# Attention on one core: the order of all steps from a new search, longer products on GpSimd, its casts under VectorE's SBUF steps, and bits and factors in rings

## The chip, the core and the metric

The kernel runs on one core of one Trainium2 chip. The metric is the device time of one execution in microseconds, here the median of 3 runs of the kernel before. The engines are called as the profile calls them: PE is TensorE (with PEld, its weight loads), DVE is VectorE, ACT is ScalarE, POOL is GpSimd, SP is SyncE, which issues most transfers.

## The reference

Grouped-query attention without a mask: 8 batches, 8 query heads and 2 key/value heads, 1,024 positions, 64 columns. That makes 64 query heads ("heads" below), four of which share one key/value head.

```python
q: (8, 8, 1024, 64)   k, v: (8, 2, 1024, 64)   # float32, drawn with deviation 0.1
scores = (1 / sqrt(64)) * q_group @ k_group.transpose
attn = exp(scores - scores_max);  attn = attn / (sum(attn) + 1e-8)
output = attn @ v_group
```

The kernel leaves the maximum out (the scores are small) and divides after the second product: a column of ones beside v gives the sum.

## The kernel before, in words

**Tiles of scores.** Keys are cut into 8 chunks of 128, so a head has 8 score tiles of 128 keys by 1,024 queries; there are 512 in all. PE makes a tile with two matmuls of 512 columns (L761) into one of three PSUM slots of two banks each (`sp`). A slot is free again when its tile has been read.

**Two ways to the exponential.** 368 tiles go to ACT, one instruction each (L771, "exponential"), which writes bf16 tiles `pt`. The other 144 go to VectorE, which makes the exponential from bits. Its steps, with the names used below:

- *pass* (L783): scores from PSUM, scaled and shifted, written as 16-bit whole numbers `yt`, 1,024 columns a tile
- *bits* (L792): the low seven bits of `yt` and a fixed exponent, to `zt`
- *exponent* (L800): the high bits of `yt`, to `et`
- *product* (L810 on VectorE, L739 on GpSimd): `zt = yt * zt`, read as bf16; the columns are split between the two engines, GpSimd takes pieces from the end ("parts")
- *sum* (L816): `zt = et + zt`, only in the last three heads; elsewhere PE adds `et` and `zt` by using both as weights

Bits, exponent and product run on a *chain* of two tiles (2,048 columns), SBUF to SBUF. Each chain has three buffers of its own, from pools of 6 (`yt`), 8 (`et`) and 8 (`zt`).

**Second product.** PE multiplies `pt`, `et` and `zt` (128 queries at a time, as weights) with v and its column of ones (L829; L849 for the first head, L869 for the last), 65 columns an instruction, into two PSUM banks in turn (`ops`). Seven query pieces of 128 fill a bank. VectorE then takes the *reciprocal* of the sums (L894) and *normalizes* (L904) into `ost`, and SP stores a head when it is complete (L913).

**Loads.** GpSimd casts q, k and v from float32 to bf16 in DRAM with DMAs of its own queue (L519, two heads of q or one batch of k or v a time). SP transposes q and k into SBUF from there (L588, L578) and copies v (L571).

**What sets the order.** Every engine runs its list in order. The lists come from a planner (class `Plan`), which walks through a string of letters, `ORDER`, with a cost for each step, and gives each step a time; it also decides on GpSimd's parts by the room that it sees under VectorE's PSUM steps (`gpsimd`, L207) and on the time of the casts (`due`, L159). The events are sorted by these times and emitted. Waits follow from the data. Two kinds are added by hand: a part of GpSimd waits until the VectorE step ahead of the latest SBUF step has ended (`gate`), and a one-column memset (`tick`, L734) takes a chain's waits for its buffers ahead of its first part.

Of the kernel before, what the change touches and what calls it, by code (L numbers as in the profile page):

```python
# [10 lines left out]
M_START = 5450  # L11
M_KREST = 50
M_SWAP = 650
M_Q1 = 3400
M_QSTEP = 2700
M_WARM = 6400
M_V0 = 8000
M_DUMMY = 110
M_SEE = 51
M_PAIR = 226  # L20
M_PTAIL = 205
M_SWITCH = 99
M_MM = 30.3
M_PVTAIL = 180
M_ACT = 917
M_ATAIL = 107
M_FIX = 66
M_DTAIL = 80
M_DEP = 34
M_D1 = 1.042  # L30
M_D2 = 0.521
M_D4 = 0.261
M_REC = 115
M_GLEAD = -55
M_GDMA = 20
M_ZLEAD = 33
M_GFIX = 190
M_GCOL = 1.88
M_GOVER = 65
M_GLATE = 900  # L40
M_GFREE = 85
M_ISSUE = 850
M_OVER = 5000
NEED = 5150
M_NORM = 531


INF = float("inf")
PB = 7
# [3 lines left out]
CHN = 2  # L53
LONG = 6
GFROM = 2
GTO = 5
GMIN = 64
GREST = 64
GSTEP = 8
STEPS = (("zh", M_D4), ("two", M_D4), ("mul", M_D2), ("add", M_D2))  # L60


ORDER = """
AaApFFFFWWWWFFAWWWWWWWWWWWWWWWWWWWWaWWWWWWWWWWApEEWWEA0bWWWApEFFWWWAW0WWWaEpAEWWA0WWAWWWWWWAFFF0FE0E
WW0WbAWWWWWWWWApWWWWWWWWWWWWAWWRWWnWaWWRWWWPWWAVVVVVVAnb0VVVApVVVVVVA0WaVApVVVVVVVA0AV0bVRVVPVVVAVVV
nVVAb0WWWWApVVVVVVVVAR0WbWWWA0VVVVPVVVVAVVVnVVA0bWWWApVVVVVVVVAR0bWWWA0VVVVPVVVVAVVVnVVA0bWWWApVVVVV
VVVA0AW0WWbVV0VVVVVARPVVVVVVAnWWbWAipVVVVVVVVA1cWWWApVVVVVVVVAr1bWWWA0VPVVVVVVAWWnWWWcWA1VVVVVpVVVAV
VVVRV1AcnWWWAVpVVVVVAVV01VAc1VVVVpVVAVVVVVRA0cWWWWAPVVVVVVVVAnWbWWWA1VVVVpVVAVVVVVRV1VAcnWWWAVpVVVVV
VVA2WWcWWAVpVVVVVVVARWW0nWcWAVpVVVVVVVA1WcWWApVVVVVVVVA00cWWWAVVVVV0VAVRVPVVVAVVVVnVVAA0VVVV1VVVVVVV
1cAV0VVVVVVVRApVVVVVVVAnWcWWAipVVVVVVVVA1cWWWApVVVVVVVVAR0b0WWWAVPVVVVVVVAnWWcWWA1VVVVpVVVVAVVVRV1Ac  # L70
WnWWWWWAVpVVVVVVVA01WWcWApVVVVVVAV1VVVVVRV0AcWWWAPVVVVVVVVAncWW1WAVVVpVVVVVAVVV0VARc0VVVVPVAVVVVVVAn
cWW1WWAVVVpVVVVVVAVV0VVVVA0bWWRWWAPVVVVVVVVnVAc1WAVVpVVVVVVVAW1WWWbAVpVVVVVVVARW0nWcWWApVVVVVVVVA1Wb
WWWApVVVVVVVVA0cRV1AVPVVVVVAVVVnVAA0VVVVV1VVVVVVV0VbAVpVVVVVVAVRV1VVAc1VVVVVPAVVVVVVAnbWWW0WAVpVVVVV
VVAVVRV1VVAc1VVVVVPAVVVVVVVAnbW0WWAVpVVVVVVVArWW1WbWAVPVVVVVVVAnWWcWA1VVVVVpVVAVVVVA01AV1VVVVVVRVnbW
AVpVVVVVVVA0WWbWAVpVVVVVVVVARWW1WbWAVPVVVVVVVVAVnVb0AVpVVVVVAVVVV0VcA1VVVVApVVVVVVA1bVVrAPVVVVVVAnbW
WWW0WApVVVVVVVVA1bWWWARPVVVVVVVVVAnbWW0WAVpVVVVVVVVVA1WWbWA0VVVVVVpVVAVVVVVA0AVRV1VVAVnVVVV0VVVVVb0A
VVVVVpVVVAVVVAR0aVPVVVAVVVVVVnVAb1WWWAVpVVVVVVVVVARWW0Wa0WAVVPVVVVVVVAVnVVVA1AVVV1VVVVVVV0VbAVpVVVVV
VVVARWWnWaWAVpVVVVVVVVVA1WbWWAVpVVVVVVVVARWnWbWWAVpVVVVVVVA01WWaWA0VVVVVpVVVAVVVA1bVRV0pVAVVVVVVnAa1
WWWWAVpVVVVVVVAW1WWWbAVpVVVVVVVARW0WbWWAPVVVVVVVVVAnbWA1VVVV0VVVApVVVVVVVARWW1WbWAVPVVVVVVVVVAVnAb0V
VVVpVVVAVVVVVVrA0nAV1VVVVVVV0bWApVVVVVVVVA0WbWWWApVVVVVVVVAR1WAWWWbV0VVVVPVVVAVVVVnVAb0WWWApVVVVVVVV  # L80
A1bWWWARVPVVVVVVVAnWWbWWA0VVVV0VVVApVVVVVVAR1AVVVnVVVVa0AVpVVVVVVAV0VVVVA0bVRVPVVVAVVVVVnAa1WWWWAVpV
# [10 lines left out]
VVVVVVVVA0WbWWWApVVVVVVVArnAVV2VVVVVV1cAVpVVVVVVVVARWWnWcWAVVpVVVVVVAVV3VVAA00VV0VVVVVVVV0VVAAVVVRV0  # L92
VVVVVV0VVVVVVAanWWWWAVpVVVVVVVVARnbWAVpVVVVVVVVA0Wb0WWWApVVVVVVVVAR0AWWWb0VVVVVPVVVAVVVVnVAb0WWWAVpV
VVVVVVARWW0WAWAVVVVVV0VVVVVVVAAVnVVVVV0VVVVVVVRVA0WAVnVVVVV0VVVVVVVVVVVVVA0AVVVVVVVVVRVnVVVVaApVxVVV
AVVVV0VVVVVRVAnAWA0VV0VVVVVVVV0VVLLRLnLLLLLFFRFn
"""


# [849 lines left out]
```

## Time and profile before

| what | value |
|---|---|
| median of 3 runs | 352.83 us (352.61 to 352.95) |
| span of the profiled execution, first to last instruction | 350.8 us |
| median over that span | 2.0 us |
| granted clock of TensorE | 0.998 |
| busy: PE, DVE, ACT, POOL | 342.2, 340.5, 342.3, 276.9 us |
| exponentials on ACT | 368, busy 339.8 us |
| first exponential starts, last one ends | 6.05 and 345.95 us |
| passes on DVE | 144, busy 174.9 us |
| products on POOL, on DVE | 151 and 64, busy 238.3 and 39.1 us |

The page shows the span of the profiled execution; what lies outside its first and last instruction is seen only as the difference to the median. Busy time counts instructions that overlap on an engine once. The next instruction on VectorE or ACT starts while the one ahead still drains, so the duration of an instruction (1.22 us for a pass) is longer than the time from its start to the next start (1.13), and the latter is what it costs.

### The profile page before, as it was taken

The numbers are of one execution on the slowest core, as the hardware profiler recorded it, in microseconds if no ns is written. First come the engines' busy times: TensorE is split into PE (matmuls) and PEld (weight loads), VectorE is DVE, ScalarE is ACT, GpSimd is POOL, SyncE is SP. The second block draws the span as 40 slices with busy tenths as digits, with TensorE's granted clock in tenths as the row PEclk, the third lists the DMA queues.
The fourth block names the chain that finished last, engine by engine and source line by source line (L and its number), as shares of the span: only waits on it lengthen the run. The fifth ranks groups of instructions, "written<-read, shape, count | busy, mean of one in ns | idle before, by whom it ended". The sixth has DMA issues, their size and how long they took to land.

```text
span 350.8 us, 14254 instructions
## 1 busy us (share of the span) xinstructions
PE 342.2 (98%) x6272; PEld 224.9 (64%) x6272; DVE 340.5 (97%) x517; ACT 342.3 (98%) x372; POOL 276.9 (79%) x265
## 2 busy tenths in 40 slices
PE   7899999999999999999999999999999999999995
PEld 3466666666666666666666666666666676666674
DVE  5999999999999999999999999999999999999995
ACT  6999999999999999999999999999999999999994
POOL 3268889799999999898999998999989958982000
PEclk9999999999999999999999999999999999999999
DMA  6899766496749757769896977297767994453223
GB/s 150 121 165 167 140 120 146 84 151 139 136 92 137 148 124 134 129 132 124 125 157 120 151 138 122 64 191 135 122 127 107 170 168 119 107 122 74 69 76 109
DMA packets 96574, 44.84 MB, mean 128 GB/s; under 512 B 61168, under 2 KB 95344, under 8 KB 95728
## 3 DMA queue, kind: packets, MB, share of 16 engines
q1 hardware_dynamic: 94128, 31.34, 43.8%
q0 software_dynamic: 2096, 12.19, 26.5%
q8 instruction: 49, 0.80, 1.1%
q10 hardware_dynamic: 288, 0.39, 0.3%
q14 instruction: 13, 0.11, 0.1%
HBM read 27.13 MB, written 28.97 MB: 160 GB/s over the span
## 4 chain that ended last, share of the span: by engine, by line
PE 60%; ACT 21%; DVE 15%; issue 1%; DMA 1%; DVEq 0%
PE ops L829 32%; PE sp L761 27%; ACT pt L771 21%; DVE yt L783 8%; DVE et L800 2%; DVE ost L904 2%; DVE zt L792 1%; DVE zt L810 1%; DMA q<-in_q_dram 1%; PE sp L869 1%; DVE rec L894 1%; PE sp L644 0%; DVE qt L662 0%; ACT q L633 0%; DVEq L943 0%
## 5 line engine op out<-in xcount | busy, mean ns | idle before, releaser
L771 ACT ACTIVATE pt<-sp 128x1024 bf16<-128x1024 f32 x368 | 339.8, 1036 | 0.5 <-PE sp L761 0.3
L739 POOL TENSOR_TENSOR zt<-yt,zt 128x560 bf16<-128x560 bf16 (+15 forms) x151 | 238.3, 1583 | 28.3 <-DVE zt L792 10.1
L829 PE MATMUL ops<-va,pt 128*128 128x65 bf16 x2840 | 177.0, 194 | 0.0
L783 DVE TENSOR_SCALAR yt<-sp 128x1024 uint16<-128x1024 f32 x144 | 174.9, 1215 | 1.3 <-PE sp L761 1.2
L761 PE MATMUL sp<-qt,kt 64*128 64x512 bf16 x1024 | 168.9, 382 | 3.2 <-ACT pt L771 1.7
L829 PEld LDWEIGHTS <-pt 128*128 128x128 bf16 x2840 | 131.5, 97 | 32.8 <-issue 32.8
L829 PE MATMUL ops<-va,zt 128*128 128x65 bf16 x1128 | 131.1, 194 | 0.0
L829 PE MATMUL ops<-va,et 128*128 128x65 bf16 x1096 | 125.3, 194 | 0.0
L829 PEld LDWEIGHTS <-et 128*128 128x128 bf16 x1096 | 87.9, 98 | 15.2 <-issue 15.0
L829 PEld LDWEIGHTS <-zt 128*128 128x128 bf16 x1128 | 91.2, 97 | 9.6 <-issue 9.2
L761 PEld LDWEIGHTS <-kt 64*128 64x128 bf16 x1024 | 50.9, 93 | 59.0 <-issue 36.0
L792 DVE TENSOR_SCALAR zt<-yt 128x2048 uint16<-128x2048 uint16 (+1 forms) x73 | 49.8, 683 | 0.5
L800 DVE TENSOR_SCALAR et<-yt 128x2048 uint16<-128x2048 uint16 (+1 forms) x73 | 49.0, 675 | 0.0
L904 DVE TENSOR_TENSOR ost<-ops,rec 128x448 f32<-128x448 f32 (+2 forms) x73 | 44.7, 612 | 0.5
L810 DVE TENSOR_TENSOR zt<-yt,zt 128x928 bf16<-128x928 bf16 (+17 forms) x64 | 39.1, 611 | 0.0
L519 POOL DMA_DIRECT2D qd<-in_q_dram x33 | 21.6, 655 | 4.4 <-PE sp L761 3.6
L894 DVE RECIPROCAL rec<-ops 128x7 f32<-128x7 f32 (+2 forms) x73 | 14.5, 199 | 0.1
L734 POOL MEMSET tick<- 128x1 bf16 x57 | 12.0, 211 | 0.0
L519 POOL DMA_DIRECT2D kd<-in_k_dram x8 | 5.3, 657 | 5.1 <-PE sp L761 5.1
L621 PE MATMUL ops<-warm 128*128 128x128 bf16 (+1 forms) x24 | 4.6, 334 | 1.2 <-DVE warm L513 1.2
L519 POOL DMA_DIRECT2D vd<-in_v_dram x8 | 5.6, 700 | 0.0
L621 PEld LDWEIGHTS <-warm 128*128 128x128 bf16 x24 | 2.0, 114 | 3.5 <-issue 2.3
(39 smaller groups left out, 27.4 us busy)
## 6 DMA issues: line engine op xcount, KB each, us to landing
out_dram<-ost SPq DMA_DIRECT2D x63, 256.0 KB, 3.1
qd<-in_q_dram POOLq DMA_DIRECT2D x29, 256.0 KB, 5.0
kt<-kt SPq DMA_DIRECT2D x30, 64.0 KB, 3.4
va<-vd SPq DMA_DIRECT2D x30, 64.0 KB, 3.1
kd<-in_k_dram POOLq DMA_DIRECT2D x7, 256.0 KB, 4.5
vd<-in_v_dram POOLq DMA_DIRECT2D x7, 256.0 KB, 5.3
qt<-qd SPq DMA_TRANSPOSE x63, 4.5
qd<-in_q_dram POOLq DMA_DIRECT2D x5, 128.0 KB, 4.0
```

What stands on the lines that cost most here:

```text
L519: return nc.gpsimd.dma_start(out=t.rearrange("(a x) d -> a (x d)", a=128), in_=src.rearrange("(a x) d -> a (x d)", a=128),)
L734: early = nc.gpsimd.memset(tick, 0.0)
L739: begun[j] = gps = nc.gpsimd.tensor_tensor(out=z, in0=flat(yt[j])[:, lo : lo + w], in1=z, op=ALU.mult)
L761: now = nc.tensor.matmul(sps[x][:, half, :], lhsT=t[lo : lo + D, c // NH, ci % NH * 128 : (ci % NH + 1) * 128], rhs=qt[j][lo : lo + D, 0, ...
L771: exps.append(nc.scalar.activation(out=p, in_=where_s[(j, c)], func=AF.Exp, scale=scale))
L783: vec = nc.vector.tensor_scalar(out=yt[ch][:, i, :, :], in0=where_s[c], scalar1=EXP_A, scalar2=EXP_B, op0=ALU.mult, op1=ALU.add,)
L792: vec = nc.vector.tensor_scalar(out=zt[j][:, 0:c], in0=yt[j][:, 0:c], scalar1=0x7F, scalar2=0x3F00, op0=ALU.bitwise_and, op1=ALU.bitwise_or,)
L800: vec = ins = nc.vector.tensor_scalar(out=et[j][:, 0:c], in0=yt[j][:, 0:c], scalar1=0x7F80, scalar2=None, op0=ALU.bitwise_and,)
L810: vec = nc.vector.tensor_tensor(out=z, in0=flat(yt[j])[:, 0 : cols[0]], in1=z, op=ALU.mult)
L829: ended[job] = nc.tensor.matmul(ops[plan.group_of[x] % 2][:, lo : lo + D + 1], lhsT=p[:, qs * 128 : (qs + 1) * 128], rhs=va[(b * G + h // ...
L894: vec = nc.vector.reciprocal(out=to, in_=sums)
L904: vec = nc.vector.tensor_tensor(out=to, in0=src, in1=by, op=ALU.mult)
```

## The change

The planner goes. A new string `ORDER`, found by another search, holds the finished order of everything: each score tile with its slot, each exponential, each VectorE step with the chain that it works on, each part of GpSimd with its length in units of 8 columns, and each cast, transpose, copy and store. A loop over its letters emits the instructions directly; two places of it:

```diff
+m2v3A0t2xVVVVVzVTVe1xA2G2,192rpVVVVVxVVVA0nd1xA2pSVVVTVVxVVA0m2q28A1t2xVV
+VVVzVCVe2xG2,195A0rpVVVVVxVVVA1ne2TxA0pSVVVVVxVVVA0m3k7A1zxVVVVVVt4VTVe2xG3,201A0
```

`A` and `a` to `g` are score tiles for ACT and VectorE (the letter counts heads ahead), `x` an exponential, `p` a pass, `z` bits, `t` exponent, `m` VectorE's product, `+` the sum, `G` a part of GpSimd, `V` three or so matmuls of the second product, `r` and `n` reciprocal and normalization, `q`, `k` and `v` casts, `T` a transpose of q, `S` a store. A digit behind `m`, `t` or `G` counts chains back.

The core of the code:

```diff
+NYT = 22
...
-    yp = ctx.enter_context(tc.tile_pool(name="yp", bufs=NYT))
-    ep = ctx.enter_context(tc.tile_pool(name="ep", bufs=NCT))
-    zp = ctx.enter_context(tc.tile_pool(name="zp", bufs=NCT))
...
+    ye = kvp.tile([128, NYT, 2, HS], U16, name="ye")
+    zz = kvp.tile([128, NYT, 2, HS], U16, name="zz")
...
+class Chain:
+    def __init__(self, at, n):
+        self.at, first = at, at % NYT
+        self.first, self.n = first, n
+        self.cols = 1024 * n
+        self.parts = 0
+    def tiles(self, ring):
+        return ring[:, self.first : self.first + self.n]
...
+        elif kind == "z":
+            gate = vec
+            ch = Chain(nzh, lengths[len(chains)])
...
+            vec = nc.vector.tensor_scalar(
+                out=ch.tiles(zz), in0=ch.tiles(ye), scalar1=0x7F, scalar2=0x3F00,
...
+        elif kind == "G":
+            ch = chains[-1 - arg[0]]
+            w = 8 * arg[1]
+            ch.cols -= w
...
+            gps = nc.gpsimd.tensor_tensor(
+                out=z, in0=flat(ch.tiles(ye))[:, ch.cols : ch.cols + w], in1=z, op=ALU.mult
+            )
...
+        elif kind == "t":
+            gate = vec
+            ch = chains[-1 - arg[0]]
+            vec = nc.vector.tensor_scalar(
+                out=ch.tiles(ye), in0=ch.tiles(ye), scalar1=0x7F80, scalar2=None,
+                op0=ALU.bitwise_and,
+            )
```

So `yt` and `et` become one ring `ye` of 22 tiles and `zt` a ring `zz` of 22. The exponent step writes over the tile that it reads. It must therefore come after the product of its chain, VectorE's and GpSimd's, where it had a buffer of its own before. Chains have one or two tiles (`LENGTHS`: 69 of two, 6 of one). The numbers of steps: 368 exponentials and 144 passes as before, 75 bits and 75 exponent steps (73 and 73), 68 products on VectorE with 45,616 columns (64 with 57,912), 95 parts on GpSimd with 101,840 (151 with 89,544), sums over 8 tiles (5), 6,234 matmuls (6,272).

**VectorE in the middle of the program.** Before, around the normalization of one bank; `yt`, `zt` and `et` are the chain's buffers, `sp` a slot of scores, `ops` a bank of the second product, and the brackets hold the semaphores that an instruction waits on (PE, Pool for GpSimd, DVE for VectorE itself, DMA queues):

```order
L783 TENSOR_SCALAR yt<-sp_2742 128x1024 [waits PE_49]
L894 RECIPROCAL rec<-ops_2616 128x7 [waits PE_49]
L792 TENSOR_SCALAR zt<-yt 128x2048 [waits DVE_49]
L800 TENSOR_SCALAR et<-yt 128x2048
L783 TENSOR_SCALAR yt<-sp_2800 128x1024 [waits PE_49,Pool_49]
L904 TENSOR_TENSOR ost<-ops_2616,rec 128x448 [waits DVE_49]
L810 TENSOR_TENSOR zt<-yt,zt 128x640
```

The same engine in the change, over one chain:

```order
L454 TENSOR_TENSOR zz<-ye,zz 128x512
L460 TENSOR_SCALAR ye<-ye 128x2048 [waits DMAHW5_49,DVE_49,Pool_49]
L428 TENSOR_SCALAR zz<-ye 128x2048
L557 RECIPROCAL rec<-ops_2575 128x7 [waits PE_49]
L419 TENSOR_SCALAR ye<-sp_2722 128x1024 [waits PE_49]
L568 TENSOR_TENSOR ost<-ops_2575,rec 128x448 [waits DVE_49]
L419 TENSOR_SCALAR ye<-sp_2766 128x1024 [waits PE_49]
```

Bits and exponent steps that stood between the passes now stand together behind the product, and four PSUM steps stand together. The wait on GpSimd has moved from the pass to the exponent step, which now also waits on VectorE's own product ahead of it.

**GpSimd at the same places.** Before; `tick` is the one-column memset, `qd` and `kd` the casts:

```order
L739 TENSOR_TENSOR zt<-yt,zt 128x560 [waits DVE_49]
L519 DMA kd_0_2626<-in_k_dram 16x8192 [waits DMASW3_49]
L734 MEMSET tick 128x1 [waits PE_49,Pool_49]
L739 TENSOR_TENSOR zt<-yt,zt 128x848 [waits DVE_49]
L519 DMA qd_2694<-in_q_dram 16x8192 [waits DMASW4_49]
```

And in the change:

```order
L445 TENSOR_TENSOR zz<-ye,zz 128x1576 [waits DVE_49]
L172 DMA vd_0_2567<-in_v_dram 16x8192 [waits DMASW6_49]
L440 MEMSET tick 128x1 [waits PE_49,Pool_49]
L445 TENSOR_TENSOR zz<-ye,zz 128x1536 [waits DVE_49]
L172 DMA qd_2686<-in_q_dram 16x8192 [waits DMASW7_49]
```

The parts are longer and fewer, one for each chain here, and a cast stands behind a part, so that it is issued when that part has ended, which is where VectorE's product and exponent step begin.

More of the change, by code (lines that the diff above doesn't have):

```diff
@@ L1 @@
 import math
+import re
 from contextlib import ExitStack
@@ L438, with groups_of @@
+def groups_of(nj):
+    last = (nj - 1) * NPIECE
+    groups = [(0, NPIECE // 2), (NPIECE // 2, NPIECE)]
+    groups += [(i, min(i + PB, last)) for i in range(NPIECE, last, PB)]
+    return groups + [(last, last + NPIECE)]
 @with_exitstack
@@ new lines, in half @@
+    def half(j, par, ci):
+        return [p for _, p in terms(j, par, [ci])]
+    for kind, arg in re.findall(r"([A-Za-z+])([0-9,]*)", "".join(ORDER.split())):
+        arg = [int(x) for x in arg.split(",")] if arg else []
+        if kind == "X":
+            begin("q", arg[0], True)
+        elif kind == "Y":
+            begin("k", divmod(arg[0], G), True)
+        elif kind == "Z":
+            begin("v", divmod(arg[0], G), True)
+        elif kind == "q":
+            begin("q", arg[0], False)
+        elif kind in "kv":
+            begin(kind, (arg[0], 0), False)
+        elif kind == "K":
+            turn_k(*kt_next.pop(0))
+        elif kind == "C":
+            copy_k(*cp_next.pop(0))
+        elif kind == "U":
+            fill_v(*fv_next.pop(0))
+        elif kind == "I":
+            place_v(0, 0)
+        elif kind == "T":
+            turn_q(tq_next)
+            tq_next += 1
+        elif kind == "S":
+            r = place_of(st_next * NPIECE)
+            ins = nc.sync.dma_start(
+                out=rows(out[divmod(st_next, H)], st_next == 0),
+                in_=ost[:, r : r + NPIECE, :].rearrange("p (s two) d -> p s (two d)", two=2),
+            )
+            stores.append(ins)
+            st_next += 1
+        elif kind in "Aabcdefg":
+            while nxt[a] == NC:
+                a += 1
+            j, x = a + (0 if kind == "A" else "abcdefg".index(kind)), arg[0]
+            c = nxt[j]
+            nxt[j] += 1
@@ L828 @@
+            for i in range(ndone, ndone + n):
                 ci, p = every[i]
                 ended[job] = nc.tensor.matmul(
-                    ops[plan.group_of[x] % 2][:, lo : lo + D + 1],
+                    ops[g % 2][:, lo : lo + D + 1],
                     lhsT=p[:, qs * 128 : (qs + 1) * 128],
@@ L873 @@
                         start=(first and i % 4 == 0 and n == 0),
-                        stop=(j == 0 and n == len(every) - 1),
+                        stop=(left_now == 0 and n == len(every) - 1),
                         skip_group_check=True,
                     )
-        elif kind in ("rec", "norm"):
-            lo, hi = x
+            if not left_now:
+                if kind == "E":
+                    pc = NPIECE
+                    norms += groups[:2]
+                else:
+                    norms.append(groups[-1])
+        elif kind in "rn":
+            lo, hi = norms[0]
             n = hi - lo
             r = place_of(lo)
-            if lo < plan.last:
-                o = ops[plan.group_of[lo] % 2][:, 0 : n * (D + 1)]
+            if lo < last:
+                o = ops[group_of[lo] % 2][:, 0 : n * (D + 1)]
                 o = o.rearrange("p (s d) -> p s d", d=D + 1)
```

685 lines of the change are left out of this document (150 added, 535 removed).

## The prediction

> **What bounds the kernel now.** I read the page's busy shares first, then the chain of waits, then the waits by engine, and last the steps of VectorE and GpSimd in order of time.
>
> ```profile
> span 350.8 us, 14254 instructions
> PE 342.2 (98%) x6272; PEld 224.9 (64%) x6272; DVE 340.5 (97%) x517; ACT 342.3 (98%) x372; POOL 276.9 (79%) x265
> ...
> PE 60%; ACT 21%; DVE 15%; issue 1%; DMA 1%; DVEq 0%
> ```
>
> Three engines are at 97 to 98%, and the chain changes hands between them. So one busy share decides nothing, and the question is which engine has idle time inside it. The table of stretches covers the run of exponentials on ACT, from the first to the end of the last:
>
> ```profile
> core 0: us, PE busy (x) PEld busy (x) DVE busy (x) ACT busy (x) POOL busy (x), PEclk, DMA share, GB/s
> 6.05:345.95 339.90, 336.76 (x6226) 222.00 (x6223) 337.20 (x504) 339.75 (x368) 274.88 (x257) 1.00 0.72 127
> ...
> PE sp L761 <- ACT pt L771: 1.7, 5, 0.5
> DVE yt L783 <- PE sp L761: 1.2, 3, 0.5
> ```
>
> ACT is without a gap in this table, and so nearly is everything else. But a gap can hide inside an instruction that starts late while the one ahead drains. Look at where ACT is undisturbed (columns: start, duration, engine, line, operation, tiles):
>
> ```profile
> L771 ACT ACTIVATE pt<-sp 128x1024 bf16<-128x1024 f32 x368 | 339.8, 1036 | 0.5 <-PE sp L761 0.3
> ...
> 332.86 1.02 ACT L771 ACTIVATE pt<-sp 128x1024 bf16<-128x1024 f32 x1
> 339.20 2.02 ACT L771 ACTIVATE pt<-sp 128x1024 bf16<-128x1024 f32 x2
> ```
>
> From 332.86 to 339.20 seven exponentials start, 0.906 us each. Over the kernel they take 339.8/368 = 0.923. So ACT could run 368 x 0.017 = 6.3 us faster: it is held, about 2% of the time, by late scores. The change keeps 368 exponentials, so these 6.3 us are the most that ACT allows. PE loses 38 of 6,272 matmuls, too few to matter. What moves is VectorE, where a step is followed by the next at once nearly everywhere:
>
> ```profile
> 111.92 0.62 DVE L904 TENSOR_TENSOR ost<-ops,rec 128x448 f32<-128x448 f32 x1
> 112.45 0.48 DVE L810 TENSOR_TENSOR zt<-yt,zt 128x640 bf16<-128x640 bf16 x1
> 112.85 1.22 DVE L783 TENSOR_SCALAR yt<-sp 128x1024 uint16<-128x1024 f32 x1
> 113.99 0.20 DVE L894 RECIPROCAL rec<-ops 128x7 f32<-128x7 f32 x1
> 114.11 0.69 DVE L792 TENSOR_SCALAR zt<-yt 128x2048 uint16<-128x2048 uint16 x1
> 114.72 0.69 DVE L800 TENSOR_SCALAR et<-yt 128x2048 uint16<-128x2048 uint16 x1
> 115.32 1.22 DVE L783 TENSOR_SCALAR yt<-sp 128x1024 uint16<-128x1024 f32 x1
> ```
>
> From start to start: normalization 0.53, product of 640 columns 0.40, pass over scores 1.14, reciprocal 0.12, bits 0.61, exponent 0.60. There is no hole. I therefore make the sum on VectorE and hand its change to the end, as long as it stays inside ACT's 6.3.
>
> **The change, part by part.** *Product columns.* GpSimd's parts fall from 151 to 95 and carry 101,840 columns where they carried 89,544. VectorE's own product falls from 57,912 to 45,616 columns.
>
> ```profile
> L810 DVE TENSOR_TENSOR zt<-yt,zt 128x2048 bf16<-128x2048 bf16 x8 | 9.7, 1209 | 0.0
> ...
> L810 DVE TENSOR_TENSOR zt<-yt,zt 128x640 bf16<-128x640 bf16 x8 | 3.8, 476 | 0.0
> ...
> 344.40 0.69 DVE L816 TENSOR_TENSOR zt<-et,zt 128x1024 bf16<-128x1024 bf16 x1
> 345.00 0.19 DVE L894 RECIPROCAL rec<-ops 128x6 f32<-128x6 f32 x1
> ```
>
> A column costs (1209 - 476)/1408 = 0.521 ns, so 12,296 columns are **-6.40 us**. The 640-column step of 0.40 leaves 0.07 as its fixed part. There are four products more (68 for 64), and two bits and two exponent steps more (75 for 73, columns equal): eight fixed parts, **+0.55**. The last heads sum their two factors in 8 tiles instead of 5, one step of 1024 more (0.60, above) and one of 2048 (0.60 + 0.53 = 1.13): **+1.73**. Steps alone: -4.1.
>
> *Waits of VectorE on its own last step.* Here the in-place factors enter.
>
> ```profile
> 161.83 0.20 DVE L894 RECIPROCAL rec<-ops 128x7 f32<-128x7 f32 x1
> 162.06 0.62 DVE L904 TENSOR_TENSOR ost<-ops,rec 128x448 f32<-128x448 f32 x1
> 162.60 1.21 DVE L783 TENSOR_SCALAR yt<-sp 128x1024 uint16<-128x1024 f32 x1
> 163.85 0.76 DVE L792 TENSOR_SCALAR zt<-yt 128x2048 uint16<-128x2048 uint16 x1
> ```
>
> The normalization right behind its reciprocal starts 0.23 after it, not 0.12. The bits step right behind its own pass starts 1.25 after it, not 1.14. So a neighbour that depends costs about 0.117. The built program of before has 34 such neighbours (15 pass to bits, 16 reciprocal to normalization, 3 product to sum). The change has 9 of these three kinds (2, 6 and 1 exponent to sum), but the exponent step now overwrites the tile that the product reads, and in 39 places it stands right behind that product and waits for it. No row shows this wait. [...] I take 0.117, the nearest rows. (48 - 34) x 0.117 = **+1.6**; the ends are -2.9 and +2.9.
>
> [...]
>
> The exponent step also waits for GpSimd's part on its tile. I cost it at nothing: VectorE's rest of the product, some 0.34 for 520 columns, lies between, and GpSimd overlaps it by less, as the next rows show. [...] The wait that the score pass had on GpSimd is gone; nothing was seen to stand there.
>
> *Longer parts.* Of the 95 parts 47 are over 1,300 columns, typically 1,528, started under an exponent or bits step and running through reciprocal, pass, normalization, pass.
>
> ```profile
> 270.45 0.20 DVE L894 RECIPROCAL rec<-ops 128x7 f32<-128x7 f32 x1
> 270.57 1.18 DVE L783 TENSOR_SCALAR yt<-sp 128x1024 uint16<-128x1024 f32 x1
> 271.66 0.61 DVE L904 TENSOR_TENSOR ost<-ops,rec 128x448 f32<-128x448 f32 x1
> 272.19 0.30 DVE L810 TENSOR_TENSOR zt<-yt,zt 128x296 bf16<-128x296 bf16 x1
> 272.41 0.69 DVE L792 TENSOR_SCALAR zt<-yt 128x2048 uint16<-128x2048 uint16 x1
> 273.05 1.22 DVE L783 TENSOR_SCALAR yt<-sp 128x1024 uint16<-128x1024 f32 x1
> ...
> 112.62 1.42 POOL L739 TENSOR_TENSOR zt<-yt,zt 128x560 bf16<-128x560 bf16 x1
> 113.99 0.91 POOL L519 DMA_DIRECT2D qd<-in_q_dram  x1
> ...
> 270.05 2.24 POOL L739 TENSOR_TENSOR zt<-yt,zt 128x904 bf16<-128x904 bf16 x1
> 272.25 0.94 POOL L519 DMA_DIRECT2D qd<-in_q_dram  x1
> ...
> 273.25 3.44 POOL L739 TENSOR_TENSOR zt<-yt,zt 128x488 bf16<-128x488 bf16 x2
> ```
>
> The 560-column part ends at 114.04, 1.19 after the pass at 112.85 opened its window. The 904 columns end at 272.29, 1.84 after the reciprocal. That is 0.65/344 = 1.89 ns a column, so 1,528 end 1.84 + 624 x 1.89 ns = 3.02 after the reciprocal. The four steps last 0.12 + 1.09 + 0.53 + 1.14 = 2.88. The part reaches 0.14 into VectorE's next step. What does that cost? At 272.19 an overlap of 0.10 cost nothing: 296 columns took 0.22, their 0.07 + 0.15. Longer is seen here:
>
> ```profile
> 164.70 4.04 POOL L739 TENSOR_TENSOR zt<-yt,zt 128x560 bf16<-128x560 bf16 x2 [0.58 <-DVE zt L792]
> ...
> 168.60 0.73 DVE L792 TENSOR_SCALAR zt<-yt 128x2048 uint16<-128x2048 uint16 x1
> 169.25 1.21 DVE L783 TENSOR_SCALAR yt<-sp 128x1024 uint16<-128x1024 f32 x1
> ```
>
> An overlap of 0.14 (to 168.74) made the bits step 0.65 long, 0.05 over its usual 0.60. Bounds: 0 and 0.05. I take 0.03, the middle, times 47: **+1.4**, with ends 0 and 2.4.
>
> *Transfers.* GpSimd starts most of its 256 KB casts behind a part, under VectorE's product, exponent and bits steps. Their landing is early enough: each transpose that reads them is issued twelve exponentials (11 us) ahead of its first score, as before. The time goes to GpSimd itself, 0.5 to 0.9 an issue, while it would idle. From the product's start to the next window there are 0.34 + 0.12 + 0.60 + 0.61 = 1.67; part tail 0.14 and issue 0.94 fit. I take 0; the cost without this cover is the slower rival.
>
> *Rings, run of scores, end.* 22 + 22 tiles replace 12 + 16 + 16, and the margins between a tile's last reader and its next writer are over ten exponentials in the order. I cost them, and the tail with its one more sum ahead of the last eight matmuls, at nothing (0.3 either way).
>
> **Sum:** -6.40 + 0.55 + 1.73 + 1.6 + 1.4 = -1.1. The profiled span of 350.8 becomes 349.7. The shown median, 352.83, stands 2.0 above that span; I leave the 2.0 as it is: **351.7 us**.
>
> **The rivals.** *More.* The 39 waits are free, VectorE saves 4.6 more, and ACT's 6.3 just hold it: 351.7 - 4.6 = 347.1. For it: nothing is read back after the product. Against it: the program has the semaphore, and every neighbour with one in these rows pays. 9%.
>
> *No change.* VectorE's saving turns into waits for PE. It is the order that couples the three engines, and ACT's 6.3 us of lateness show that work saved on one does not reach the others by itself: 352.8. Against it: VectorE has the fewest holes of the three. 22%.
>
> *Slower.* GpSimd is late at its window. At 272.25 the issue started 0.16 before a bits step, lasted 0.94, past that step's end at 273.05, and the next part began at 273.25, 0.2 inside the pass. In the order of the change 22 casts stand between VectorE's product and an exponent or bits step. If issue and the small memset behind it are held through both steps, a 1,528-column part starts 0.2 late and reaches 0.34 into the next product, which then waits the added 0.2: 22 x 0.2 = 4.4, or 356.1; half of them 353.9. It decides from about 0.1 of lateness. Against it: at 113.99 two such steps followed, the issue took 0.91 and ended under the second, free before the window. 22%.
>
> [...]
>
> **Chances.** Forecast 47%, of which 5% end within 0.2%; more 9%; no change 22%; slower 22%. A change of 0.2%, 0.7 us, is about what this kernel's measurement can tell. Faster: 42 + 9 = 51%; same: 5 + 22 = 27%; slower 22%. The forecast's own range, from the two ends of the overlap and the tail, is 350.0 to 353.0. For 8 in 10 I take 349.8 to 354.0: below it lies the free wait, above it half of the slower rival.
>
> **What would show it.** Exponent steps 0.117 late behind their product (product of 520 columns to exponent 0.46, not 0.34); 1,528-column parts of about 3.4 us ending 0.14 into the next step; VectorE's steps adding up to 1.1 less; exponentials nearer 0.920 than 0.923 apart. Casts that end inside a pass would show the slower rival. I am wrong if VectorE shows new holes ahead of its passes, since then the order and not the work decides.

## The result, and the profile after

The change makes the kernel slower: 408.29 us (median of 4, 404.82 to 410.01) against 352.89 for the kernel before on the same chip, a ratio of 1.156 with a 95% interval of 1.151 to 1.161. The forecast was 351.7, with 349.8 to 354.0 for 8 in 10. Here and below medians are over all runs of a kernel, ratios and their intervals over its fast runs alone (those within 1.5% of its fastest), so the two can differ a little. From the page of the kernel after, its first rows and two groups, ACT's exponentials and VectorE's exponent steps (the last column is the idle time ahead of the group and what ended it):

```profile
span 403.0 us, 14111 instructions
PE 353.5 (88%) x6234; PEld 227.4 (56%) x6234; DVE 377.8 (94%) x527; ACT 346.0 (86%) x372; POOL 274.6 (68%) x206
...
L407 ACT ACTIVATE pt<-sp 128x1024 bf16<-128x1024 f32 x368 | 343.4, 1052 | 47.7 <-PE sp L396 46.2
...
L460 DVE TENSOR_SCALAR ye<-ye 128x2048 uint16<-128x2048 uint16 (+1 forms) x75 | 86.9, 1163 | 3.5
```

The same group, the exponent step, on the page of the kernel before:

```profile
L800 DVE TENSOR_SCALAR et<-yt 128x2048 uint16<-128x2048 uint16 (+1 forms) x73 | 49.0, 675 | 0.0
```

ACT, which idled 0.5 us ahead of its exponentials before, idles 47.7 now, 46.2 of it for scores. VectorE looks busier, 377.8 us for 340.5, and one group alone grew by 37.9: 75 exponent steps take 86.9 us, where 73 took 49.0. The waits by engine of the kernel after (us in total, times, the longest) show the way from there to ACT:

```profile
ACT pt L407 <- PE sp L396: 46.2, 33, 3.5
PE sp L396 <- DVE ye L419: 33.4, 15, 3.1
POOL zz L445 <- DVE ye L460: 27.4, 15, 5.3
...
DVE ye L419 <- PE sp L396: 12.7, 14, 2.7
```

Some 15 times PE waits up to 3.1 us for a pass of VectorE to free a slot of scores, ACT then waits for PE, GpSimd for the exponent step, and VectorE's next passes for PE in turn. It is not spread evenly. Of the table of stretches of 20 us (busy time and instructions of PE, PEld, DVE, ACT and POOL, then granted clock), one undisturbed and one with such waits:

```profile
120.00:140.00 20.00, 19.92 (x375) 13.07 (x372) 19.74 (x31) 19.95 (x23) 19.78 (x14) 1.00 0.74 117
200.00:220.00 20.00, 15.51 (x270) 9.93 (x267) 19.80 (x22) 14.86 (x16) 12.17 (x9) 0.91 0.42 83
```

In the second one VectorE is "busy" for 19.80 us and makes 22 steps where it made 31. Something holds single steps. Here is one, in VectorE's and then GpSimd's rows of the kernel after:

```profile
177.65 0.68 DVE L428 TENSOR_SCALAR zz<-ye 128x2048 uint16<-128x2048 uint16 x1
178.25 0.45 DVE L454 TENSOR_TENSOR zz<-ye,zz 128x560 bf16<-128x560 bf16 x1
178.79 3.61 DVE L460 TENSOR_SCALAR ye<-ye 128x2048 uint16<-128x2048 uint16 x1
182.32 0.19 DVE L557 RECIPROCAL rec<-ops 128x7 f32<-128x7 f32 x1
```

```profile
177.71 0.72 POOL L172 DMA_DIRECT2D qd<-in_q_dram  x1
178.43 0.12 POOL L440 MEMSET tick<- 128x1 bf16 x1
178.78 3.07 POOL L445 TENSOR_TENSOR zz<-ye,zz 128x1528 bf16<-128x1528 bf16 x1 [0.23 <-DVE zz L454]
```

The exponent step lasts 3.61 us instead of 0.69. It ends at 182.40, 0.55 after the end of GpSimd's part of 1,528 columns beside it (181.85), as if it had done its work only behind the part. Part and step were released by the same thing, the end of VectorE's product; the part started at 178.78, the step at 178.79. Twelve exponent steps take 3.5 to 3.7 us and one 2.5; together they are 36.9 us too long. (The thirteen were picked out by their durations; the difference of the two groups' rows, 37.9, is nearly all theirs.) In the twelve the part starts 5 to 26 ns ahead of the step. In the thirteenth the issue of a cast and a memset stand ahead of the part; it starts 0.155 us behind the step (265.89 and 265.74), and the step is held all the same.

Such a race had been decided the other way in the kernel before. There a bits step right behind its own pass and a part released by the same pass also start together, and the step wins; VectorE's row and GpSimd's:

```profile
82.57 0.69 DVE L792 TENSOR_SCALAR zt<-yt 128x2048 uint16<-128x2048 uint16 x1
```

```profile
82.62 1.75 POOL L739 TENSOR_TENSOR zt<-yt,zt 128x560 bf16<-128x560 bf16 x1 [0.31 <-DVE yt L783]
```

So the theory is: **the two engines race for something that only one can have for the whole length of an instruction (below: the port), and in the change GpSimd wins 13 races.** The rows agree: an exponent step of the same shape takes 0.69 us, and 3.61 beside a part of 3.07. They do not show what decides who is first when both wait for the same event; the runs below do.

### The profile page after: what moved, and what is told of

The parts are those of the page before. It is cut to its first block, busy times and chain, and to the rows that moved or that the text cites. A ratio compares the mean times of both kernels' runs of the same rounds, so it can differ in the third digit from the quotient of the medians.

```text
span 403.0 us, 14111 instructions
## 1 busy us (share of the span) xinstructions
PE 353.5 (88%) x6234; PEld 227.4 (56%) x6234; DVE 377.8 (94%) x527; ACT 346.0 (86%) x372; POOL 274.6 (68%) x206
## 5 line engine op out<-in xcount | busy, mean ns | idle before, releaser
L407 ACT ACTIVATE pt<-sp 128x1024 bf16<-128x1024 f32 x368 | 343.4, 1052 | 47.7 <-PE sp L396 46.2
L445 POOL TENSOR_TENSOR zz<-ye,zz 128x1528 bf16<-128x1528 bf16 (+23 forms) x95 | 235.1, 2476 | 94.7 <-DVE ye L460 27.4
L419 DVE TENSOR_SCALAR ye<-sp 128x1024 uint16<-128x1024 f32 x144 | 174.4, 1211 | 13.1 <-PE sp L396 12.7
L488 PE MATMUL ops<-va,pt 128*128 128x65 bf16 x2864 | 171.6, 198 | 0.0
L488 PE MATMUL ops<-va,zz 128*128 128x65 bf16 x1104 | 124.5, 196 | 0.0
L488 PE MATMUL ops<-va,ye 128*128 128x65 bf16 x1072 | 119.9, 196 | 2.6 <-DVE ye L460 2.6
L488 PEld LDWEIGHTS <-ye 128*128 128x128 bf16 x1072 | 83.7, 99 | 16.4 <-issue 13.6
L488 PEld LDWEIGHTS <-zz 128*128 128x128 bf16 x1104 | 86.5, 99 | 9.7 <-issue 9.7
L460 DVE TENSOR_SCALAR ye<-ye 128x2048 uint16<-128x2048 uint16 (+1 forms) x75 | 86.9, 1163 | 3.5
L428 DVE TENSOR_SCALAR zz<-ye 128x2048 uint16<-128x2048 uint16 (+1 forms) x75 | 49.4, 663 | 0.1
L454 DVE TENSOR_TENSOR zz<-ye,zz 128x520 bf16<-128x520 bf16 (+21 forms) x68 | 33.6, 495 | 0.0
```

Source lines behind the costliest of these rows:

```text
L407: exps.append(nc.scalar.activation(out=p, in_=where_s[(j, c)], func=AF.Exp, scale=scale))
L419: vec = nc.vector.tensor_scalar(out=ye[:, i, :, :], in0=where_s[(j, c)], scalar1=EXP_A, scalar2=EXP_B, op0=ALU.mult, op1=ALU.add,)
L428: vec = nc.vector.tensor_scalar(out=ch.tiles(zz), in0=ch.tiles(ye), scalar1=0x7F, scalar2=0x3F00, op0=ALU.bitwise_and, op1=ALU.bitwise_or,)
L445: gps = nc.gpsimd.tensor_tensor(out=z, in0=flat(ch.tiles(ye))[:, ch.cols : ch.cols + w], in1=z, op=ALU.mult)
L454: vec = nc.vector.tensor_tensor(out=z, in0=flat(ch.tiles(ye))[:, 0 : ch.cols], in1=z, op=ALU.mult)
L460: vec = nc.vector.tensor_scalar(out=ch.tiles(ye), in0=ch.tiles(ye), scalar1=0x7F80, scalar2=None, op0=ALU.bitwise_and,)
```

## Experiments: the lost port

Four kernels repair or leave the suspected races. *First*, a part that follows an exponent step right behind its own product waits for that exponent step (`late`) instead of for the step ahead of it:

```diff
-            tc.add_manual_dep(gps.ins, gate.ins.name, Sync, reason="the port goes to the step behind it")
+            behind = late if late else gate
+            tc.add_manual_dep(gps.ins, behind.ins.name, Sync, reason="the port goes to the step behind it")
```

> One edit to the change: where the exponent step stands right behind its own product, GpSimd's next part waits for that exponent step and no longer for the product ahead of it. Theory (the port is lost): part and exponent step wait for the same event, the end of the product, and in 13 places the part starts 5 to 26 ns first and holds the exponent step for some 2.9 us; with the edit all 75 exponent steps last about 0.69 us, 38 us of blocked time go, and the time falls to 352 to 357 us. Rival (the new order or the longer parts themselves don't fit: VectorE and PE wait for each other): blocked steps go, but the time stays above 385 us because the holes move elsewhere.

Measured: 365.12 us, ratio to before 1.026 (1.019 to 1.034). *Second*, the exponent is not in place, so that it waits for no step of its own engine:

```diff
-                out=ch.tiles(ye), in0=ch.tiles(ye), scalar1=0x7F80, scalar2=None,
+                out=ch.tiles(ee), in0=ch.tiles(ye), scalar1=0x7F80, scalar2=None,
```

> The change with the exponent step not in place: it writes to a ring of its own, so that it waits neither for the product ahead of it nor for GpSimd; order, part lengths and what a part waits for are those of the change (rings of 14, 18 and 18 tiles and 30 tiles for ACT, so that it fits). Theory (the port is lost because the in-place step waits): no exponent step is blocked, a step behind its product starts 0.12 us sooner, 350 to 355 us. Rival (what a part waits for is at fault, whatever the exponent step does): 13 steps stay blocked, about 400 us.

Measured: 361.87, ratio 1.017 (1.008 to 1.026). *Third*, bits and exponent exchanged where no part stands between, and *fourth*, this with the first repair (letters of other engines left out):

```diff
-m0 t0 z
+m0 z t1
```

> The change with bits and exponent step exchanged in the 20 places where product, exponent step and bits stand in a row with no part between, so that the exponent step no longer follows its own product. If the waits of VectorE on its own last step were the loss, 20 of 39 of them go and about half of the 55 us with them (380 us). Theory (the port is lost only where a part follows directly): these 20 places were never blocked, the gain is 20 x 0.11 = 2 us, 403 to 409 us.

> Both edits: bits and exponent step exchanged in 20 places, and parts wait for the exponent step where it still stands right behind its product. Theory: as with the second edit alone, less 20 x 0.11 us on VectorE: 350 to 355 us, 1 to 2 us under the second edit alone. Rival (order or long parts don't fit): above 385 us.

Measured: 408.67, ratio 1.157 (1.153 to 1.160), for the exchange alone; 361.29, ratio 1.021 (1.014 to 1.027), with the repair. In the first, second and fourth kernel no exponent step is held as before (their groups take 50.1, 49.8 and 49.7 us); in the third the thirteen still are. Exchanging steps changes nothing; taking the race away by either of two independent means brings 46 to 49 of the 55 us back, by the ratios. But the three expectations, 350 to 357 in all, were missed by 6 to 8 us: a second cause is left, and is taken up below.

**Who wins.** Before this run I thought: whoever needs an extra instruction for its waits loses. A step that waits for several semaphores keeps one of them and has the others on a separate instruction ahead of it; the trace of the change has 67 such instructions at its 75 exponent steps. So I put waits on the exponent steps of the kernel before, where nothing is in place. With one added wait:

```diff
+            tc.add_manual_dep(ins.ins, gate.ins.name, Sync, reason="its own engine's last step")
```

> The kernel before, in which every exponent step waits in addition for VectorE's step right ahead of it, the same step that a GpSimd part behind it waits for. Nothing else is moved. 46 of the 73 exponent steps have a part behind them; 27 of these wait for a DMA as well, so that the wait on two or three semaphores needs an instruction of its own, and 19 wait for VectorE alone. Theory of the lost port, with the extra instruction as what decides: the 27 are held for their whole part (their parts last 46.0 us together, less 0.15 each: 42 us), the 19 are not; with some 4 us for the waits themselves, 390 to 402. If a wait on the same step is enough to lose, all 46 are held: 76 us more, 420 to 435. Rival, that the port is not lost by such a wait and the change's time came from its order: 354 to 360.

And with a second one, on a part of GpSimd that ended long before:

```diff
+            if gps is not None:
+                tc.add_manual_dep(ins.ins, gps.ins.name, Sync, reason="GpSimd's last part")
```

> As the run with the one added wait, and every exponent step waits in addition for GpSimd's last part, which ended before: now nearly all have two or more semaphores and the extra instruction. Theory of the lost port decided by the extra instruction: nearly all 46 steps with a part behind them are held, together some 76 us: 415 to 435, and some 30 more than the run with the one wait. If the number of semaphores does not matter: the same time as the run with the one wait, within 5 us.

Measured: 359.98 (1.020, 1.019 to 1.022) with one wait, 425.93 (1.207, 1.205 to 1.210) with two. The group of the exponent steps in the first and in the second:

```profile
L800 DVE TENSOR_SCALAR et<-yt 128x2048 uint16<-128x2048 uint16 (+1 forms) x73 | 50.1, 687 | 2.5
```

```profile
L800 DVE TENSOR_SCALAR et<-yt 128x2048 uint16<-128x2048 uint16 (+1 forms) x73 | 109.9, 1506 | 6.7 <-DVE zt L792 0.5
```

The first result goes against my expectation of 390 to 402: none of the 46 steps with a part behind them is held, though 27 of them do have the extra instruction; their parts start 44 to 117 ns behind the step. By its time alone it is what the rival gave, that such a wait loses no port; the second run decides against that. The second came out as expected: all 46 are held, 60 us together, also seven whose recorded start is 12 to 31 ns ahead of the part's. The built programs show the difference:

```
one wait, a step with a DMA:   ahead of the step: DMA          on the step: DVE
two waits, the same step:      ahead of the step: DMA, DVE     on the step: Pool
```

So the extra instruction alone does no harm. What counts is **which wait stands on it**. If the wait on VectorE, the one that decides the race, is on the step itself, the step wins (46 of 46 in the first run); if it is on the instruction ahead, the step behind that instruction comes too late (46 of 46 in the second). In the change the exponent step waits for VectorE, for GpSimd and some for a DMA, and the wait on GpSimd is the one that stays on the step.

This can be tried on the change itself. VectorE's product takes the wait on GpSimd, and the exponent step behind it has none left; the parts' waits stay as they are:

```diff
+            if ch.at in begun:
+                tc.add_manual_dep(vec.ins, begun[ch.at].ins.name, Sync, reason="the tile's part has ended")
```

> The change, in which VectorE's product waits for the GpSimd parts of its tile, so that the exponent step behind it has no wait on GpSimd left and waits for VectorE (and some for a DMA) alone: the wait on VectorE then sits on the step itself and not on an instruction ahead of it. Which step GpSimd's part waits for is left as the change has it. Theory: the step now wins the port in all 13 places: 408 less some 40 = 363 to 372 (the late transpose of the start remains, and the product's new wait costs up to 0.2 in some 50 places). If a wait on the same step is enough to lose the port, 400 or more.

Measured: 364.50, ratio 1.035 (1.028 to 1.042), as expected. No exponent step is held any more; the group in this kernel:

```profile
L462 DVE TENSOR_SCALAR ye<-ye 128x2048 uint16<-128x2048 uint16 (+1 forms) x75 | 49.8, 668 | 1.3
```

That settles the first cause: 408.3 to 364.5 by moving a wait that had long ended where it stood from the exponent step to the product ahead of it.

## Experiments: the start

What is left in the kernel with the first and third edits, 361.29 us? Its waits, and the stretches of 3 us in which they lie (PE, PEld, DVE, ACT and POOL busy, then the granted clock):

```profile
DVE ye L420 <- PE sp L396: 9.1, 4, 7.0
ACT pt L407 <- PE sp L396: 8.8, 3, 7.9
...
PE sp L396 <- DMA qt<-qd: 8.2, 1, 8.2
```

```profile
18.00:21.00 3.00, 0.00 (x0) 0.00 (x0) 1.55 (x5) 1.15 (x2) 2.20 (x2) 0.63 1.12 103
21.00:24.00 3.00, 0.00 (x0) 0.00 (x0) 0.00 (x0) 0.00 (x0) 1.89 (x2) 0.50 1.40 54
24.00:27.00 3.00, 1.05 (x6) 0.22 (x7) 0.41 (x1) 0.00 (x0) 0.00 (x0) 0.50 1.10 172
27.00:30.00 3.00, 3.00 (x44) 2.12 (x44) 1.33 (x3) 2.21 (x3) 0.00 (x0) 0.66 0.41 98
30.00:33.00 3.00, 2.66 (x51) 1.64 (x48) 2.95 (x6) 3.00 (x4) 0.66 (x1) 1.00 0.58 120
```

One transposed q is late, once, by 8.2 us, and all engines stop. The change issues GpSimd's casts of the start closer together: a pair of k heads and q heads 4 to 11 within 3 us, where the kernel before spreads them over 22. I moved three of them back (`Y2`, `X8` and `X10` are casts of k heads and of q heads 8 and 10 on, `K` the transpose of a k head), and as the reverse put them together in the kernel before:

```diff
-x A2 p Y2 E0 ... X4 X6 X8 K ... m0 x q10 b0 ... G0,72 p T T T
+x A2 p E0 ... X4 X6 K ... m0 x b0 ... G0,72 Y2 X8 p T T T ... t1 X10 x
```

> The kernel with both repairs (bits and exponent exchanged in 20 places, the part waiting for the exponent step that stands right behind its own product), in which in addition three of the first casts (the second pair of k heads, q heads 8 and 9, q heads 10 and 11) are issued where the kernel before has them: after the first two parts, and the third some 14 us later. Theory of the start: in the kernel with both repairs PE waits 8.2 us for one transposed q in the stretch 20 to 40, because the cast that it reads was issued with four others of 256 KB and lands with them; ACT is 8.9 us behind the kernel before by 40 us (27.7 us busy for 36.5). Moved apart, the wait goes and the time falls by 8 to 9, to 351 to 354. Rival: the remaining 8 us lie in the steady part (lower clock, parts that reach into the next step); then it stays at 358 to 362.

```diff
+    ev.insert(of(("cq",), 4), ev.pop(of(("ck",), (1, 0))))
+    for j in (10, 8):
+        ev.insert(of(("cq",), 6) + 1, ev.pop(of(("cq", "q"), j)))
```

> The kernel before, with the same three casts pulled forward to where the change has them, directly around the casts of q heads 4 to 7. Theory of the start: the transposed q of heads 4 on is late by 3 to 8 us and the kernel takes 355 to 362. Rival (the casts' place does not matter, and the late transpose belongs to the other changes): 352 to 354.

Measured: 355.52 (1.009, 1.006 to 1.012) for the first, so 4 to 6 us are back (by the ratios, and by the medians). The reverse did nothing: 353.01 (1.002, 0.999 to 1.005). So the bunch alone is not the cause. The kernel before also has another order on SP's queue; I tried that order alone, and with the casts (`U` fills a v head):

```diff
-X8 K A2 x T m0 ... v1 V T ... V V V V U x
+X8 T K A2 x m0 ... v1 V U T ... V V V V x
```

> The kernel with both repairs of the lost port, with the casts as the change has them, in which two transfers of the start are exchanged on SP's queue as the kernel before has them: the transpose of q head 3 ahead of that of the second k head, and the fill of the second v head ahead of the transposes of q heads 8 and 9. Theory of SP's order: the kernel before with the casts pulled forward lost nothing, so the bunch of casts alone is not the cause; the transpose of q head 3 is issued behind the k head's, into the bunch of casts, and lands 14 us later. Put ahead, the 8 us wait of PE goes: 351.5 to 355. Rival (the bunch of casts holds whatever transpose comes next): 358 to 362.

> As the run with SP's order, and the three casts moved apart as well. If SP's order and the bunch of casts must come together to do harm, this is as fast as the run with SP's order alone, 351.5 to 354, and below the run with the casts alone (355.5), which still waited for the fill of v behind the transpose of q head 9. If VectorE's 4 us of shorter steps count once nothing is late, 349 to 351.

Measured: 359.30 (1.017, 1.012 to 1.022) and 356.13 (1.010, 1.007 to 1.013). SP's order alone is not told from 361.29 either. How long the transposes of q took to land in the first 36 us (shortest, median, longest), first in the kernel before as it is, and with the bunch put into it:

```profile
DMA to landing us min/median/max: 2.5/6.1/7.3
```

```profile
DMA to landing us min/median/max: 2.4/3.0/5.3
```

Then in the kernel with both repairs, in the one with SP's order alone, and in the last one:

```profile
DMA to landing us min/median/max: 2.5/4.3/13.8
```

```profile
DMA to landing us min/median/max: 2.4/4.3/17.5
```

```profile
DMA to landing us min/median/max: 2.4/5.0/9.8
```

The medians tell nothing; the longest do. In the kernel before with the bunch, the transpose of q head 3 is issued at 9.5, the bunch begins at 10.5, and it lands after 2.4 us. In the kernel with SP's order it is issued at 10.0, but the bunch has begun at 8.8 with the pair of k heads; it lands 17.5 us later, and in the kernel with both repairs, issued at 12.1 into the same bunch, 13.8 us later. In these traces a transpose issued into a bunch of five casts takes 7 to 17 us; of one issued ahead of such a bunch there is the one case of 2.4. (Ahead of a pair of casts, in the kernel before as it is, it took 6.7.) I did not find what sets the spread, so this part is not shown as a cause. And the change has less time to spare: it scores heads ahead of their turn, head 7 before heads 5 and 6, so that the transpose of head 7 must land some 7 us after its issue where the kernel before leaves 15.

Next I spread four more casts (`Z2`, `X10`, `X12`, `X14`; `Z2` is one of v heads), in this kernel and in the one whose exponent has a ring of its own:

```diff
-... V V m0 v1 ... A2 m0 q12 A1 ... q14 ...
+... A1 C Z2 x ... d0 X10 x ... e0 X12 x ... d0 X14 x
```

> The change with everything found so far mended: both repairs of the lost port, SP's order and the three casts of the start as in the run before, and four more of GpSimd's casts (the third pair of v heads, q heads 10 to 15) issued about as far apart as the kernel before has them, one after each second part or so, from 26 to 42 us. Theory of the bunched casts: the transposes of q heads 6 to 9 landed 8 to 10 us after their issue in the run with the casts moved apart, because five casts were issued between 17.7 and 23.0; in the kernel before the same take 5 to 7. Without the bunch ACT has no gap in its first 40 us, the 4.8 us it was behind are gone, and the time is 351 to 353.5. If VectorE's shorter steps then count for their full 4 us, 348 to 350; if they count for nothing because ACT and PE have no slack either, 352.5 to 353.5. Rival (the slow landings come from something else): 355 to 357.

> The same mending of the transfers, on the kernel in which the exponent has a ring of its own and waits for nothing on its own engine (order and parts' waits as the change has them). VectorE saves the waits of some 40 exponent steps on their product as well, some 4 us more than in the run beside it. If VectorE is what bounds once nothing is late, this is 3 to 5 below the run beside it; if ACT and PE bind, the two are equal within 1.

Measured: 358.31 (1.014, 1.012 to 1.016) and 356.44 (1.010, 1.008 to 1.012), no better. The transposes were in time now, but I had made a new hole. VectorE's row and GpSimd's in the first of the two:

```profile
45.94 2.28 DVE L456 TENSOR_TENSOR zz<-ye,zz 128x152 bf16<-128x152 bf16 x1
```

```profile
44.15 0.71 POOL L172 DMA_DIRECT2D qd<-in_q_dram  x1
44.86 0.49 POOL L172 DMA_DIRECT2D kd<-in_k_dram  x1
45.36 2.75 POOL L446 TENSOR_TENSOR zz<-ye,zz 128x432 bf16<-128x432 bf16 x2
```

Two casts side by side, 1.2 us, pushed GpSimd's parts behind their window, and a product of 152 columns, 0.15 us by its columns, took 2.28. This is the prediction's rival *Slower*, met in my own edit. One cast moved to a place where GpSimd idles:

```diff
-d0 X14 x p S
+p G1,53 X14 x
```

> As the run with everything mended, but the cast of q heads 14 and 15 stands ahead of a part of 1,464 columns where GpSimd idles 1.1 us, not next to the cast of the third pair of k heads. In that run the two casts side by side (1.2 us) pushed a part of 432 columns behind its window; it began at 45.4, VectorE's product at 45.94 took 2.28 instead of some 0.15, and ACT had a gap of 1.6 at 48.0 and 2.2 more by 56. Theory: that hole goes, all else is as there: the gaps over the kernel before were 4.8, of which some 4 stood there, so 352.5 to 354. Rival (the casts are spread and it is the order of the change that leaves holes elsewhere): 356 to 358.

> The same move of one cast in the kernel in which the exponent has a ring of its own. Its gap of 1.6 at 47.5 goes: 352 to 354. If VectorE bounds where nothing is late, 348 to 351.

Measured: 354.31 (1.005, 1.004 to 1.007) and 354.21 (1.004, 1.002 to 1.005). With the races and the start mended, 54 of the 55 us are back, and no version of the change came below the kernel before. The same 240 us of the steady part, in the kernel before and in the first of these two:

```profile
60.00:300.00 240.00, 239.25 (x4418) 157.53 (x4417) 239.23 (x359) 239.96 (x261) 220.36 (x207) 1.00 0.76 132
```

```profile
60.00:300.00 240.00, 238.41 (x4445) 157.17 (x4442) 238.37 (x361) 239.84 (x262) 211.84 (x156) 1.00 0.74 133
```

261 exponentials and 262: the same pace. The 1.5 us that remain lie at the two ends: the 41st exponential starts 1.3 us later than in the kernel before, the last one 0.9 later, and what follows the last takes 5.4 us for 4.8. And the second kernel of the pair, which saves VectorE the waits of some 39 exponent steps besides (with shorter rings), is as fast as the first within 0.1 us by the medians; the intervals overlap. So VectorE's savings do not reach the end, and that was the premise of the forecast.

## Experiments: what a saving on VectorE is worth

The premise by itself, in the kernel before:

```diff
-            z = flat(zt[j])[:, 0 : cols[0]]
+            w = cols[0] * 79 // 800 * 8
+            z = flat(zt[j])[:, 0:w]
```

> The kernel before, in which each of VectorE's own products covers only 79% of its columns (45,504 of 57,912; the rest of the products is left out and stays undone). VectorE loses 12,408 columns of 0.521 ns, 6.5 us, nearly what the change took off it (6.4), and nothing else is touched: order, parts, casts, waits. The forecast's premise, that VectorE's saving reaches the end as long as ACT allows it: 345.5 to 348.5. Rival No change (the order couples three engines of which two have no slack): 351.5 to 353.

Measured: 352.75, ratio 0.9996 (0.9988 to 1.0005). Its busy shares, ACT's group and VectorE's wait:

```profile
PE 342.4 (98%) x6272; PEld 225.4 (64%) x6272; DVE 336.5 (96%) x517; ACT 342.2 (98%) x372; POOL 273.5 (78%) x265
...
L771 ACT ACTIVATE pt<-sp 128x1024 bf16<-128x1024 f32 x368 | 339.7, 1036 | 0.3 <-PE sp L761 0.2
...
DVE yt L783 <- PE sp L761: 3.8, 12, 0.6
```

VectorE has 6.5 us less to do by its columns (its busy time falls by 4.0), waits 3.8 us for PE where it waited 1.2, and the exponentials still take 339.7/368 = 0.923 each. Nothing arrives. Then PE, and both:

```diff
+                if i == 3 and piece % 2:
+                    continue
```

> The kernel before, in which PE leaves out 248 of its matmuls over the probabilities, one in every odd piece of 128 queries (their terms are missing from the sums); everything else is untouched. They follow each other by some 0.032 us (eight in 0.42, the last 0.19 long), so PE has some 8 us less to do. If PE binds the steady part together with nothing else, the time falls by ACT's 6.3 us to 346 to 348. If ACT binds (its exponentials stand 0.923 apart because of what they do and not because scores are late), or if VectorE binds, 352 to 353.

> Both left out: PE's 248 matmuls and VectorE's 12,408 product columns. VectorE alone was worth nothing. If PE alone moves the time, this equals the run with PE alone; if the two only count together, 346 to 349 here and 352 to 353 there; if ACT binds, 352 to 353 in both, and no work taken off any engine but ACT could have made this kernel faster.

Measured: 351.64 (0.9960, 0.9946 to 0.9975) and 351.35 (0.9949, 0.9933 to 0.9965). Neither expectation was met exactly; PE's 8 us were worth 1.3, and VectorE's 6.5 on top 0.3, which the intervals do not tell from nothing. ACT's group in the two:

```profile
L771 ACT ACTIVATE pt<-sp 128x1024 bf16<-128x1024 f32 x368 | 338.6, 1058 | 0.4 <-PE sp L761 0.2
```

```profile
L771 ACT ACTIVATE pt<-sp 128x1024 bf16<-128x1024 f32 x368 | 338.2, 1068 | 0.8 <-PE sp L761 0.6
```

0.920 and 0.919 us each. With slack on both other engines ACT hardly gets faster. Why not can be read from the traces, by matching each exponential with the second score matmul of its tile (both engines run their lists in order). Of the 367 distances from start to start in the kernel before, 154 are 0.903 to 0.912 us, in every part of the kernel and not only at its end. Here are six in a row in its middle:

```profile
178.02 1.02 ACT L771 ACTIVATE pt<-sp 128x1024 bf16<-128x1024 f32 x1
...
183.44 1.10 ACT L771 ACTIVATE pt<-sp 128x1024 bf16<-128x1024 f32 x1
```

Another 145 are about 0.920. Half of their scores had ended 0.37 us or more before; what makes them 0.017 longer is open. The other 68 are longer, up to 1.12, and each of these exponentials starts 0.04 to 0.11 us after the end of its scores: here the scores are late. One of them, ACT's rows and then PE's:

```profile
171.32 1.05 ACT L771 ACTIVATE pt<-sp 128x1024 bf16<-128x1024 f32 x1
172.41 1.02 ACT L771 ACTIVATE pt<-sp 128x1024 bf16<-128x1024 f32 x1
```

```profile
171.86 0.19 PE L829 MATMUL ops<-va,pt 128*128 128x65 bf16 x1
171.98 0.39 PE L761 MATMUL sp<-qt,kt 64*128 64x512 bf16 x2
```

PE is not idle ahead of any of the 68; in 65 of them the score matmuls stand directly behind one of the second product. What the distances have over 0.903 adds up to 7.5 us: 4.9 in the 68 and 2.5 in the 145. The late scores stay late when work is taken away: 5.0 us with the products left out on VectorE, 4.3 with the matmuls left out on PE, 4.0 with both. So I take it that mostly their place in the order makes them late; no run here moves them. What an order that puts them sooner would be worth is open.

## Why the prediction was wrong

*"The exponent step also waits for GpSimd's part on its tile. I cost it at nothing."* **This is the step that failed.** The wait itself did cost nothing. But it is one more wait of the same instruction, and it pushed the wait on VectorE's product onto an instruction of its own, behind which GpSimd's part takes the port: 13 exponent steps held, 36.9 us on VectorE and 43 to 49 us of the time (the four kernels without held steps, by the ratios; what adds the difference I did not separate). I had quoted the two rows that show all of it in the order of the change (the exponent step's three waits, and a part that waits for VectorE alone), and had looked only at when a wait is satisfied, not at which instruction is first when two engines wait for one event.

*"Waits of VectorE on its own last step", +1.6.* The kind was right, the size was too small. In the change a product of 440 columns is followed by its exponent step so:

```profile
173.12 0.40 DVE L454 TENSOR_TENSOR zz<-ye,zz 128x440 bf16<-128x440 bf16 x1
173.60 0.69 DVE L460 TENSOR_SCALAR ye<-ye 128x2048 uint16<-128x2048 uint16 x1
```

From start to start this is 0.48, and by the prediction's own 0.07 + 0.23 the wait is 0.18. Over the 42 such pairs of the trace the median is 0.17; three have none. With the wait on the step itself (the run in which the product takes the wait on GpSimd) the median is 0.12, which is the 0.117 that I took. The upper end of the term, +2.9, is 0.15 for each of the 39 waits, which no run shows; the 0.17 that the change shows makes it +3.7 instead of +1.6.

*"Transfers: I take 0."* Wrong by 5 to 7 us: 361.3 to 354.3 from the moved casts and SP's order, together (by the ratios 5.4). "Twelve exponentials ahead, as before" counted the order, and not that a transpose issued into a bunch of casts landed 7 to 17 us later.

*Longer parts, +1.4.* Not tested by itself. A part of 1,528 columns beside VectorE's passes took 3.46, as I said (about 3.4); where it held an exponent step it took 3.07. The steady part of the mended kernel runs at the pace of the kernel before.

*Product columns, fixed parts, sums, -4.1, and "I make the sum on VectorE and hand its change to the end, as long as it stays inside ACT's 6.3".* The second half is the other step that failed. Taking the same 6.5 us off VectorE alone moved the time by 0.0 (interval -0.4 to +0.2). The reading of the 6.3 us as late scores was right for the larger part: 4.9 us are. But it does not follow that less work on VectorE brings scores sooner: 5.0 us of lateness remained without VectorE's 6.5, and 4.0 without PE's 8 as well, when the time fell by 1.6. So even without the races the forecast, faster, would have been wrong. The rival *No change* comes nearest to the mended kernel (352.8, and 354.3 measured), and for the reason that it gave: the order couples the engines, and work saved on VectorE turned in part into waits for PE.

*The rivals.* *More* asked for free waits; they cost 0.17 each, and in the kernel without them nothing was gained. *Slower* had the right pair, a late part of GpSimd that holds a step of VectorE, but in the change a cast makes little of it: eight of the 95 parts start directly behind the issue of a cast, seven of them within 0.16 us of the end of the bits step ahead and without a step held for their whole length; only the thirteenth held step has a cast ahead of its part. And the price of a lost port is not the 0.2 us of lateness but the whole part, 2.9 us for an exponent step beside a part of 3.07. It came to that in the run with two casts side by side, 2.1 us for one product.

*What would show it.* "New holes ahead of its passes" did appear, 12.7 us in 14 waits for PE where the kernel before had 1.2 in 3, but PE was late there because VectorE was. The larger loss stood inside VectorE's exponent steps, as busy time. A step that is blocked counts as busy: the group's mean of 1163 ns against 675 was the sign, not a wait.

## What to carry to other kernels

When two engines can hold each other's steps, as a part of GpSimd held VectorE's exponent step here (3.61 us for 0.69), and wait for the same event, ask which of the two instructions carries that wait itself: an added wait, even one long satisfied, can move it to an instruction ahead, as the one on GpSimd did here, and the step is then held for the length of the other's instruction. Here the loss showed as a group whose mean duration grew (1163 ns for 675), and not among VectorE's waits. And before work is moved off an engine, leave that work out by itself and time it, although the kernel then no longer computes everything: if the time does not move, the move is worth nothing in this order of steps, however well it is done.

## What the runs showed of the hardware that I had not expected

- Who wins a race of 0.01 us is not chance: 46 of 46 exponent steps lost it with the deciding wait on the instruction ahead, 0 of 46 with it on the step.
- A dependent neighbour on VectorE cost 0.12 us (median) with its wait on the step, in the run in which the product takes the wait on GpSimd, and 0.17 with it on an instruction ahead, in the change.
- A transpose that SP issued into a bunch of five of GpSimd's casts landed after 7 to 17 us; the one issued 1 us ahead of such a bunch took 2.4.
- Exponentials of 1,024 columns start 0.903 us apart at best, in all parts of the kernel before, and 145 of its 367 distances are 0.920 though their scores are there; what makes the 0.017 is open.
- In the kernel with the first and third edits the granted clock fell to 0.50 about 1 us after PE's last matmul, which ended at 17.76 (0.63 on average from 18 to 21 puts the fall at 18.8, if it was one step), and was whole again at 29.0, 3 us after PE had begun again at 25.95 (0.66 on average from 27 to 30); so the first 3 us behind the hole ran at half the clock too.
